# The second mixer with part of GpSimd's elementwise work on other engines, and the router in column tiles

## The chip, the cores and the metric

The kernel runs on one core of a Trainium2 chip: five engines (TensorE for matmuls, here PE; VectorE, DVE; ScalarE, ACT; GpSimd, POOL; SyncE, SP, which only issues transfers) work in order, each on its own queue, and wait for one another by semaphores. The metric is device microseconds (us) for one execution, lower is better.

## The reference

Two layers of a diffusion block on 512 latent rows and 256 context rows of width 1024. Layer 0 mixes by latent attention and retention, layer 1 by a two-directional RWKV-7 recurrence and a window attention; after each mixer a router picks rows for 16 experts (expert choice) and a gated feed-forward layer adds their outputs. What the change touches:

```python
p = p + mu * (0.5 * (left_neighbour + right_neighbour) - p)   # rwkv_features, per column of p
w = -softplus(-(w0[d] + tanh(wl) @ w2[d])) - 0.5
a = sigmoid(a0[d] + al @ a2[d])
key = k * (1 + (a - 1) * k_a)
S = S * dec + (S @ -kk) (kk * a)^T + v k^T                      # one step of the recurrence
aff = softmax(h @ w_router); gate, idx = top_k(aff^T, 64 or 32)   # 16 experts
```

The recurrence is computed in chunks of 64 steps; inside a chunk a 64x64 unit triangular matrix T = I + G is inverted by doubling blocks, once per head.

## The kernel before

Order of the work: mixer 0, router 0, experts of layer 0, mixer 1, router 1, experts of layer 1. Weights of the experts stream through a ring of 2 MB slots. The framework places the instructions of each engine by its own planner, with tile releases as waits, except on PE in the expert layers, where the order is that of the program.

Mixer 1 (mixer1, from L791) is one static loop that steps many generators in turn:

- `front` projects the input: for each block of 128 columns of the weight matrix, `weights` (L863) loads 512 KB, ACT rounds it to a high part (L871), and DVE or POOL in turn subtracts it to get the low part (L872); `project` (L919) does 24 matmuls (L926). `shifted` (L929) turns the result `pb` into the shifted feature: ACT copies it between two zero columns (L937), POOL adds the left and right neighbours (L939), DVE or ACT scales by 1-mu (L941, L943), DVE adds hm times the sum (L944). It runs 25 times, on 256 or 512 columns.
- `features` (L950), 12 times on 256 columns, makes decays and keys: ACT's tanh (L972), on POOL the step to a sigmoid (L975), the factor of the key (L1009) and its product with k (L1014), on DVE a scan (L996) and the products that go to DRAM (L1021 to L1031), from where they are loaded again.
- `prep` (L1295), 24 times (2 directions, 2 halves of the heads, 6 row tiles), solves the triangular systems of four chunks. DVE masks the Gram matrix into `GA` (L1331) and adds I into `Thbd` (L1338); POOL makes `Ttbd` = GA - I (L1341) and the first masked block `Zbd` (L1357); DVE transposes (L1356) and masks (L1358) X; then come five levels of matmul, copy and transpose (L1285, L1366 to L1384). At the end the residual is formed on PE (L1398, L1399: T X + I for each of four chunks) and used to correct the inverse; POOL rounds a copy to half precision (L1393).
- `chain` (L1416), 48 steps in four independent strands, carries the state: POOL multiplies the old state by the decay (L1428), PE, DVE, ACT (L1443) and PE make the update, DVE joins them (L1452).
- `win_attend`, `finish` and `projected` (L1556 to L1563) follow in the same loop.

The router (`route_open` L1654, `route_tile` L1664) norms a row tile, transposes and scales it (`ht`), and forms 16 logits with 8 matmuls, each with 128 rows of `ht` as the stationary operand and 16 columns moving. The router's weights `wr` lie in a pool that lives through the whole kernel:

```python
        lg = self.bank("lg")
        for k in range(8):
            nc.tensor.matmul(lg[:, 0:16], ht[:, k], self.rwr[:, k], start=k == 0, stop=k == 7)   # L1688
        nc.vector.tensor_copy(self.lgt[:, t], lg[:, 0:16])
```

Of the kernel before, what the change touches and what calls it, by code (L numbers as in the profile page):

```python
# [11 lines left out]
F32 = mybir.dt.float32  # L12
# [3 lines left out]
AF = mybir.ActivationFunctionType  # L16
# [83 lines left out]
class Kern:  # L100
# [690 lines left out]
    def mixer1(self):  # L791
# [69 lines left out]
        def weights():  # L861

            while len(cut) < 2 and (queue or order):  # L863
# [8 lines left out]
                (nc.vector if len(order) % 2 else nc.gpsimd).tensor_tensor(w[:, 1], raw, w[:, 0].bitcast(F32), OP.subtract)  # L872
# [9 lines left out]
        nc.gpsimd.tensor_copy(id16[:, 0:128], self.ident)  # L882
        nc.gpsimd.tensor_copy(id16[:, 128:192], id64)
# [46 lines left out]
        def shifted(blk, a, out):  # L930

            n = a[0].shape[2]
            for pb in project(a, 1024 // n):
                yield
            pd = fo.tile([128, NLAT + 2], F32, name="pd")
            nc.gpsimd.memset(pd[:, 0:n + 2:n + 1], 0.0)
            nc.scalar.activation(pd[:, 1:n + 1], pb, AF.Copy)  # L937
            s = fo.tile([128, NLAT], F32, name="sh")
            nc.gpsimd.tensor_tensor(s[:, :n], pd[:, 0:n], pd[:, 2:n + 2], OP.add)  # L939
            if n < NLAT or blk % 2:  # L940
                nc.vector.tensor_scalar(out, pb, om[:, blk:blk + 1], None, OP.mult)  # L941
            else:
                nc.scalar.activation(out, pb, AF.Copy, scale=om[:, blk:blk + 1])  # L943
            nc.vector.scalar_tensor_tensor(out, s[:, :n], hm[:, blk:blk + 1], out, OP.mult, OP.add)  # L944
# [6 lines left out]
        def features(p, t0, kp, rp, vp, low):  # L951
# [13 lines left out]
            for (lst, wt, src, bias) in ((sig, w2, tl, w0v), (aa, a2, al, a0v)):  # L965
# [7 lines left out]
                if lst is sig:  # L973
                    for d in dirs:
                        nc.gpsimd.tensor_scalar(sig[d], sig[d], 0.5, 0.5, OP.mult, OP.add)  # L975
# [31 lines left out]
            for d in dirs:  # L1007
                nc.vector.scalar_tensor_tensor(q0[d], aa[d], 1.0, kk, OP.add, OP.mult)
                nc.gpsimd.tensor_scalar(aa[d], aa[d], hka[:, p:p + 1], oka[:, p:p + 1], OP.mult, OP.add)  # L1009
# [3 lines left out]
            for d in dirs:  # L1013
                nc.gpsimd.tensor_tensor(aa[d], aa[d], kp, OP.mult)  # L1014
# [280 lines left out]
        def prep(sl, st_, d, u, j):  # L1295
# [44 lines left out]
            for h in range(2):  # L1340
                nc.gpsimd.tensor_tensor(Ttd[h], GA[0:64, :, h], id64[0:64, None, :].to_broadcast([64, 4, 64]),  # L1341
                                        OP.subtract)
# [12 lines left out]
            for h in range(2):  # L1355
                nc.vector.transpose(X[hd[h]], Thd[h])  # L1356
                nc.gpsimd.tensor_tensor(Zd[h], Thd[h], lev(0, 1 - d)[hd[h]], OP.mult)  # L1357
# [58 lines left out]
        def chain(d, u, j):  # L1416
# [7 lines left out]
            for c in ((0, 1) if d == 0 else (1, 0)):  # L1424
                n0 = Ns[c] = N0[d, u]
                dec = PL[:, d, 2 * u:2 * u + 2, 2 * tt + c]
                n0s = rf.tile([128, 2, 64], F32, name="n0s", tag=f"s{d}{u}", bufs=1)
                nc.gpsimd.tensor_tensor(n0s, n0, dec[:, :, None].to_broadcast([128, 2, 64]), OP.mult)  # L1428
# [22 lines left out]
                for p in range(2):  # L1451
                    nc.vector.scalar_tensor_tensor(N1[:, p], a2_(pn)[:, p], dec[:, p:p + 1], n0s[:, p], OP.mult, OP.add)  # L1452
# [201 lines left out]
    def route_open(self, l):  # L1654
# [497 lines left out]
```

## Time and profile before

| | |
|---|---|
| median of 3 runs | 2968.59 us (2965.43 to 2972.07) |
| the profiled execution | 2972.21 us, its span 2970.4 us |
| busy: PE, DVE, ACT, POOL | 2660.2 us (90%), 1322.9 us (45%), 742.6 us (25%), 471.4 us (16%) |
| mean granted TensorE clock | 0.954 |
| chain that ended last, by engine | PE 64%, DMA 19%, DVE 9%, POOL 3%, ACT 3% |

Busy shares are averages over stages with different limits. The chain that ended last is followed back from the last instruction, at each step to what released it; time of an engine on it is time that set the end. "issue" in it is time without a wait that the profile shows. A matmul of 4-byte operands leaves two records in the trace.

### The profile page before, as it was taken

Reading aid. Unit: us, or ns where it says so; the run is one execution under the profiler, and the core shown is the slowest. Engines: PE = TensorE matmul, PEld = TensorE weight load, DVE = VectorE, ACT = ScalarE, POOL = GpSimd, SP = SyncE. Lnnn points to the kernel's source line nnn. Section 1 sums busy time; section 2 is a strip of 40 time slices with the busy share of each in tenths; the row PEclk is TensorE's granted clock in tenths of the full one; section 3 lists DMA queues with packets and bytes.
Section 4 is the critical chain, followed back from the end, with each engine's and each line's share of the span. In section 5 each row is a group of like instructions: output and inputs, shape, how many; then the busy total and the mean of one; then the engine's idle time right before and its main releaser. Section 6 shows DMA issues by size and latency. Waiting matters only on the chain.

```text
span 2970.4 us, 47837 instructions
## 1 busy us (share of the span) xinstructions
PE 2660.2 (90%) x19606; PEld 1535.4 (52%) x19606; DVE 1322.9 (45%) x3546; ACT 742.6 (25%) x1718; POOL 471.4 (16%) x591
## 2 busy tenths in 40 slices
PE   7999999799999999999878878799987987888886
PEld 4787776544444444444466656587653332333322
DVE  4323665444234334322475777677654332223312
ACT  3212444211111111101354544366321111101111
POOL 2332003200000000000283553411210000000000
PEclk9999999799999999999987988899987999999999
DMA  9765001488988988988642233310349999999997
GB/s 329 244 246 175 27 12 57 172 333 353 371 356 355 371 345 367 365 355 355 216 126 73 86 108 120 111 32 28 118 184 377 426 427 427 427 426 427 426 427 314
DMA packets 176587, 779.47 MB, mean 262 GB/s; under 512 B 24327, under 2 KB 110768, under 8 KB 133488
## 3 DMA queue, kind: packets, MB, share of 16 engines
q1 hardware_dynamic: 169200, 752.31, 64.5%
q0 software_dynamic: 3872, 12.52, 1.2%
q10 hardware_dynamic: 3296, 11.58, 1.0%
q8 instruction: 155, 2.54, 0.4%
q14 instruction: 64, 0.52, 0.1%
HBM read 745.68 MB, written 30.67 MB: 261 GB/s over the span
## 4 chain that ended last, share of the span: by engine, by line
PE 64%; DMA 19%; DVE 9%; POOL 3%; ACT 3%; issue 2%; SPq 0%; POOLq 0%; ACTq 0%; DVEq 0%
PE gu L1924 13%; PE ydn L1992 9%; DMA wd<-in_moe_w_down_dram 8%; DMA we<-in_moe_w_gate_up_dram 8%; PE guc L1937 6%; PE ydc L1996 3%; PE pj L926 3%; PE pj L411 2%; PE pj L412 2%; PE pj L413 2%; PE op L774 2%; PE op L1556 2%; PE adap L231 2%; PE sc L593 1%; PE scp L1816 1%
## 5 line engine op out<-in xcount | busy, mean ns | idle before, releaser
L1924 PE MATMUL gu<-we,xs 128*64 128x512 f32 x3072 | 687.9, 597 | 83.5 <-DMA we<-in_moe_w_gate_up_dram 83.4
L1924 PEld LDWEIGHTS gu<-we,xs 128*64 128x64 f32 x3072 | 216.7, 137 | 520.5 <-issue 408.5
L1992 PE MATMUL ydn<-wd,uT 128*64 128x512 f32 x1536 | 351.8, 600 | 14.3 <-DMA wd<-in_moe_w_down_dram 13.7
L1930 DVE TENSOR_TENSOR sg<-gu,sg 64x512 f32<-64x512 f32 x96 | 66.5, 693 | 458.4 <-ACT sg L1929 457.8
L1929 ACT ACTIVATE sg<-gu 64x512 f32<-64x512 f32 x96 | 56.8, 592 | 846.3 <-PE gu L1924 846.3
L1776 POOL DMA_INDIRECT xg<-xnd,idx x22 | 20.9, 952 | 1246.6 <-DVE gate L1781 1186.0
L1992 PEld LDWEIGHTS ydn<-wd,uT 128*64 128x64 f32 x1536 | 107.9, 137 | 205.3 <-issue 187.0
L1937 PE MATMUL guc<-we,xs 128*32 128x256 f32 x3072 | 172.6, 380 | 0.0
L926 PE MATMUL pj<-aL,wblk 128*128 128x512 f32 x504 | 158.1, 448 | 0.0
L1937 PEld LDWEIGHTS guc<-we,xs 128*32 128x32 f32 x3072 | 96.4, 110 | 68.4 <-issue 7.5
L411 PE MATMUL pj<-ah,wblk 128*128 128x384 f32 (+1 forms) x320 | 109.5, 343 | 1.4 <-ACT ah L380 1.4
L926 PEld LDWEIGHTS pj<-aL,wblk 128*128 128x128 f32 x504 | 99.0, 210 | 18.4
L412 PE MATMUL pj<-al,wblk 128*128 128x384 f32 (+1 forms) x320 | 107.9, 338 | 0.0
L413 PE MATMUL pj<-ah,wblk 128*128 128x384 f32 (+1 forms) x320 | 107.4, 336 | 0.0
L1819 DVE TENSOR_TENSOR x<-scp,x 128x512 f32<-128x512 f32 x144 | 92.3, 684 | 30.3 <-PE scp L1817 29.4
L1996 PE MATMUL ydc<-wd,uTc 128*32 128x256 f32 x1536 | 90.6, 380 | 1.4 <-DMA wd<-in_moe_w_down_dram 1.4
L1906 DVE COPY uTc<-utc 128x128 f32<-128x128 f32 x48 | 14.0, 291 | 172.6 <-PE utc L1904 172.1
L2046 DVE TENSOR_TENSOR yp<-ydn,gbc 64x512 f32<-64x512 f32 x64 | 44.1, 689 | 103.8 <-PE ydn L1992 103.3
L1796 DVE TENSOR_SCALAR xs<-xst,gm,modT 128x128 f32<-128x128 f32 (+1 forms) x88 | 34.8, 397 | 118.9 <-PE xst L1788 115.7
L1900 ACT ACTIVATE uT<-utp 128x256 f32<-128x256 f32 x96 | 36.0, 375 | 159.4 <-PE utp L1899 158.6
L1382 DVE STREAM_TRANSPOSE Zbd<-X 64x256 f16<-64x256 f16 x144 | 62.7, 436 | 24.2 <-ACT X L1376 21.8
L1996 PEld LDWEIGHTS ydc<-wd,uTc 128*32 128x32 f32 x1536 | 47.6, 110 | 43.9 <-issue 15.2
(421 smaller groups left out, 4630.4 us busy)
## 6 DMA issues: line engine op xcount, KB each, us to landing
we<-in_moe_w_gate_up_dram SPq DMA_DIRECT2D x192, 2048.0 KB, 13.5
wd<-in_moe_w_down_dram SPq DMA_DIRECT2D x95, 2048.0 KB, 11.8
adaw<-in_ada_w_dram SPq DMA_DIRECT2D x48, 1024.0 KB, 6.5
wraw<-in_od_w_in_dram SPq DMA_DIRECT2D x33, 512.0 KB, 4.2
wraw<-in_ev_w_in_dram SPq DMA_DIRECT2D x19, 512.0 KB, 6.8
fb<-B SPq DMA_DIRECT2D x24, 256.0 KB, 2.5
BK<-fb SPq DMA_DIRECT2D x24, 256.0 KB, 3.0
xnd<-xn ACTq DMA_DIRECT2D x10, 512.0 KB, 4.7
```

Of the source, the lines that this page charges most:

```text
L231: nc.tensor.matmul(pb[32 * j:32 * j + 32], self.spad[:, k, :], w[:, 512 * j:512 * j + 512], start=k == 0, stop=k == 7, tile_position=(0, 3 ...
L411: nc.tensor.matmul(pb[:m, :384], w[:, 0, k, 0:m], ah[k][:, t], start=k == 0, stop=False)
L412: nc.tensor.matmul(pb[:m, :384], w[:, 0, k, 0:m], al[k][:, t], start=False, stop=False)
L413: nc.tensor.matmul(pb[:m, :384], w[:, 1, k, 0:m], ah[k][:, t], start=False, stop=k == 7)
L926: nc.tensor.matmul(pb[:, :n], w[:, i, k], a[j][:, k], start=k + i + j == 0, stop=k == 7 and i == 1)
L1382: nc.vector.transpose(Zd[h], X[hd[h]])
L1819: nc.vector.tensor_tensor(xs, pb, xs, OP.add)
L1924: nc.tensor.matmul(gu[64 * j:64 * j + 64, :], g.xs[:, k, 64 * a:64 * a + 64], ws[j][k], start=k == 0, stop=k == 7, tile_position=(0, 64 * j))
L1930: nc.vector.tensor_tensor(sg, gu[64:128], sg, OP.mult)
L1937: nc.tensor.matmul(guc[32 * j:32 * j + 32, 0:256], q.xs[:, k, 32 * a4:32 * a4 + 32], ws[j // 2][k][:, 256 * (j % 2):256 * (j % 2) + 256], ...
L1992: nc.tensor.matmul(y[64 * h:64 * h + 64, :], uT[:, f], wt[i][:, 512 * h:512 * h + 512], start=f == 0, stop=f == 11, tile_position=(0, 64 * h))
L1996: nc.tensor.matmul(yc[32 * j:32 * j + 32, 0:256], uTc[:, f], wt[i][:, 256 * j:256 * j + 256], start=f == 0, stop=f == 11, tile_position=(0 ...
```

## The change

Every elementwise operation of mixer 1 that stood on POOL in the loops above goes to DVE or ACT, or falls away: the low part of the weights always on DVE; the neighbour sums as two multiply-adds of DVE straight from the matmul's bank; the two affine steps of `features` on ACT and the product on DVE; `Ttbd` a plain copy on ACT, with the subtraction of I done by PE; the masked `Zbd` on DVE; the half-precision copy on ACT; the decayed state no longer formed, since (new + old) is multiplied by the decay. The router's 8 matmuls become 8 in column tiles, 32 wide, with `ht` moving, and one that adds the four tiles up and transposes; its weights move to the router's own pool.

```diff
-                (nc.vector if len(order) % 2 else nc.gpsimd).tensor_tensor(w[:, 1], raw, w[:, 0].bitcast(F32), OP.subtract)
+                nc.vector.tensor_tensor(w[:, 1], raw, w[:, 0].bitcast(F32), OP.subtract)
...
+        minus = cpl.tile([128, 128], F32, name="minus")
+        nc.scalar.activation(minus, self.ident, AF.Copy, scale=-1.0)
...
-            pd = fo.tile([128, NLAT + 2], F32, name="pd")
-            nc.gpsimd.memset(pd[:, 0:n + 2:n + 1], 0.0)
-            nc.scalar.activation(pd[:, 1:n + 1], pb, AF.Copy)
-            s = fo.tile([128, NLAT], F32, name="sh")
-            nc.gpsimd.tensor_tensor(s[:, :n], pd[:, 0:n], pd[:, 2:n + 2], OP.add)
-            if n < NLAT or blk % 2:
-                nc.vector.tensor_scalar(out, pb, om[:, blk:blk + 1], None, OP.mult)
-            else:
-                nc.scalar.activation(out, pb, AF.Copy, scale=om[:, blk:blk + 1])
-            nc.vector.scalar_tensor_tensor(out, s[:, :n], hm[:, blk:blk + 1], out, OP.mult, OP.add)
+            nc.scalar.activation(out, pb, AF.Copy, scale=om[:, blk:blk + 1])
+
+            for o, s in ((1, 0), (0, 1)):
+                o = out[:, o:n - 1 + o]
+                nc.vector.scalar_tensor_tensor(o, pb[:, s:n - 1 + s], hm[:, blk:blk + 1], o, OP.mult, OP.add)
...
-                        nc.gpsimd.tensor_scalar(sig[d], sig[d], 0.5, 0.5, OP.mult, OP.add)
+                        nc.scalar.activation(sig[d], sig[d], AF.Identity, bias=half, scale=0.5)
...
-                nc.gpsimd.tensor_scalar(aa[d], aa[d], hka[:, p:p + 1], oka[:, p:p + 1], OP.mult, OP.add)
+                nc.scalar.activation(aa[d], aa[d], AF.Identity, bias=oka[:, p:p + 1], scale=hka[:, p:p + 1])
...
-                nc.gpsimd.tensor_tensor(aa[d], aa[d], kp, OP.mult)
+                nc.vector.tensor_tensor(aa[d], aa[d], kp, OP.mult)
...
-                nc.gpsimd.tensor_tensor(Ttd[h], GA[0:64, :, h], id64[0:64, None, :].to_broadcast([64, 4, 64]),
-                                        OP.subtract)
+                nc.scalar.activation(Ttd[h], GA[0:64, :, h], AF.Copy)
...
-                nc.gpsimd.tensor_tensor(Zd[h], Thd[h], lev(0, 1 - d)[hd[h]], OP.mult)
+                nc.vector.tensor_tensor(Zd[h], Thd[h], lev(0, 1 - d)[hd[h]], OP.mult)
...
-            nc.gpsimd.tensor_copy(Zc, Zf)
+            nc.scalar.activation(Zc, v3(pz), AF.Copy)
...
+            nc.tensor.matmul(v3(pf), id16[:, 0:128], id16[:, None, 128:192].to_broadcast([128, 4, 64]), start=True,
+                             stop=False)
+            nc.tensor.matmul(v3(pf), minus, X, start=False, stop=False)
             for c in range(4):
-                o = pf[:, 64 * c:64 * c + 64]
-                nc.tensor.matmul(o, Tt[:, c], X[:, c], start=True, stop=False)
-                nc.tensor.matmul(o, id16[:, 0:128], id16[:, 128:192], start=False, stop=True)
+                nc.tensor.matmul(pf[:, 64 * c:64 * c + 64], Tt[:, c], X[:, c], start=False, stop=c == 3)
...
-                nc.gpsimd.tensor_tensor(n0s, n0, dec[:, :, None].to_broadcast([128, 2, 64]), OP.mult)
...
-                for p in range(2):
-                    nc.vector.scalar_tensor_tensor(N1[:, p], a2_(pn)[:, p], dec[:, p:p + 1], n0s[:, p], OP.mult, OP.add)
+                nc.vector.tensor_tensor(N1, a2_(pn), n0, OP.add)
+                nc.vector.tensor_tensor(N1, N1, dec[:, :, None].to_broadcast([128, 2, 64]), OP.mult)
...
-        self.rwr = self.small.tile([128, 8, 16], F32, name="wr", tag="wr", bufs=1)
-        nc.gpsimd.dma_start(self.rwr, io["moe_router"][l].rearrange("(k p) n -> p k n", p=128))
+        self.rwr = self.rtw.tile([128, 8, 32], F32, name="wr", bufs=1)
+        nc.gpsimd.memset(self.rwr[:, :, 16:32], 0.0)
+        nc.gpsimd.dma_start(self.rwr[:, :, 0:16], io["moe_router"][l].rearrange("(k p) n -> p k n", p=128))
...
+        lp = self.bank("lgp")
+        for i in range(2):
+            for j in range(4):
+                nc.tensor.matmul(lp[32 * j:32 * j + 32, 0:128], self.rwr[:, 4 * i + j], ht[:, 4 * i + j], start=i == 0,
+                                 stop=i == 1, tile_position=(0, 32 * j))
+        ls = self.rtw.tile([128, 128], F32, name="ls")
+        nc.scalar.activation(ls, lp[:, 0:128], AF.Copy)
+        yield
+
         lg = self.bank("lg")
-        for k in range(8):
-            nc.tensor.matmul(lg[:, 0:16], ht[:, k], self.rwr[:, k], start=k == 0, stop=k == 7)
+        nc.tensor.matmul(lg[:, 0:16], ls, self.rsum, start=True, stop=True)
         nc.vector.tensor_copy(self.lgt[:, t], lg[:, 0:16])
```

`rsum` is four 16-column slices of the identity added up by DVE in `route_open`.

## Rows read from the trace of the kernel before

**Rows 1.** Busy time by stretch: PE, PEld, DVE, ACT, POOL, clock, DMA share, GB/s.
```profile
1456.00:1560.00 104.00, 72.79 (x426) 63.53 (x424) 75.17 (x139) 57.97 (x120) 74.65 (x104) 0.83 0.51 150
1560.00:1910.00 350.00, 290.11 (x2396) 221.59 (x2397) 239.43 (x533) 151.90 (x372) 160.79 (x219) 0.87 0.31 91
1910.00:2110.00 200.00, 178.16 (x2004) 152.60 (x2003) 137.43 (x416) 118.90 (x354) 41.15 (x65) 0.93 0.23 73
...
2400.00:2500.00 100.00, 84.00 (x400) 31.98 (x398) 27.14 (x80) 10.97 (x23) 0.94 (x1) 1.00 1.01 427
```

**Rows 2.** The chain that ended last, mixer 1, 1456 to 2206 us, by line.
```profile
by line: PE pj L926 10.4%; issue 5.4%; PE op L1556 4.5%; PE pe L1398 3.8%; DVE Thbd L1338 3.4%; PE sw L1200 3.2%; PE po L1236 3.1%; DVE Zbd L1382 2.5%; DVE X L1356 2.0%; PE px L1285 1.7%; POOL wblk L872 1.7%; PE pf L1285 1.7%; PE gv L1406 1
```

**Rows 3.** The same, 1456 to 1560 us.
```profile
by line: PE pj L926 13.6%; issue 8.7%; POOL wblk L872 7.4%; POOL ssq L987 4.9%; ACT wblk L871 4.7%; SPq L1312 4.6%; PE lw L969 3.7%; POOL lo L1014 3.5%; POOL lo L1009 3.4%; DVE raw L817 3.0%; DMA BK<-fb 3.0%; POOL lo L975 2.9%; DVE wblk L87
```

**Rows 4.** The same, 1560 to 1910 us.
```profile
by line: PE pj L926 18.2%; issue 5.6%; PE pe L1398 4.1%; DVE Thbd L1338 3.8%; DVE Zbd L1382 2.8%; POOL lo L1009 2.3%; DVE X L1356 2.2%; DVE cl L996 2.1%; DMA BK<-fb 2.1%; PE gv L1406 2.0%; PE pf L1285 2.0%; PE px L1285 2.0%; DMA fa<-A 1.9%;
```

**Rows 5.** The same, 1640 to 1760 us.
```profile
by line: PE pj L926 11.0%; POOL lo L1009 6.6%; DMA fa<-A 5.7%; issue 5.3%; POOL lo L1014 4.6%; DVE cl L996 4.3%; ACT lo L972 3.2%; DVE Zbd L1382 2.7%; PE lw L969 2.7%; PE pe L1398 2.7%; POOL sh L939 2.6%; DVE Thbd L1338 2.6%; POOL ssq L987 
```

**Rows 6.** Groups of POOL by form, mixer 1: busy us, mean ns, idle before.
```profile
L872 POOL TENSOR_TENSOR wblk<-wraw,wblk 128x1024 fp32r<-128x1024 f32 x17 | 42.0, 2470 | 14.4 <-ACT wblk L871 14.2
...
L1009 POOL TENSOR_SCALAR lo<-lo,hka,oka 128x256 f32<-128x256 f32 x24 | 22.4, 937 | 3.0 <-DVE t L1008 3.0
...
L1014 POOL TENSOR_TENSOR lo<-lo,ko 128x256 f32<-128x256 f32 x24 | 18.2, 772 | 0.6
```

**Rows 7.** Groups of DVE and ACT by form, mixer 1.
```profile
L1338 DVE TENSOR_TENSOR Thbd<-GA,m 64x256 f16<-64x256 f32 x48 | 35.9, 747 | 0.9
...
L872 DVE TENSOR_TENSOR wblk<-wraw,wblk 128x1024 fp32r<-128x1024 f32 x16 | 20.9, 1307 | 2.5 <-ACT wblk L871 2.3
...
L1005 DVE TENSOR_TENSOR lo<-cl,lo 128x256 f32<-128x256 f32 x24 | 9.4, 423 | 0.1
...
L944 DVE SCALAR_TENSOR_TENSOR ro<-sh,hm,ro 128x512 f32<-128x512 f32 x4 | 3.0, 746 | 0.5 <-POOL sh L939 0.5
...
L980 ACT ACTIVATE kq<-ko,vT 128x256 f32<-128x256 f32 x12 | 6.1, 511 | 3.4 <-DVE ko L944 3.4
```

**Rows 8.** Timeline of DVE in two of the 24 preps: start, us, instruction.
```profile
1883.73 1.70 DVE L1338 TENSOR_TENSOR Thbd<-GA,m 64x256 f16<-64x256 f32 x2
...
1886.74 0.28 DVE L1358 TENSOR_TENSOR X<-X,lev 128x256 f16<-128x256 f16 x1
...
1918.12 0.86 DVE L1338 TENSOR_TENSOR Thbd<-GA,m 64x256 f16<-64x256 f32 x2
```

**Rows 9.** Matmuls on the chain, in order of time: start, us, line, records.
```profile
1489.59 0.45 PE lw L969 x2
...
2081.51 1.06 PE po L1236 x10
...
2099.42 0.48 PE pe L1398 x2
```

**Rows 10.** Who waited for whom in mixer 1: us in total, times, longest.
```profile
ACT UV L1443 <- PE pu L1440: 52.5, 24, 6.6
...
PE pf L1285 <- DVE X L1358: 23.2, 16, 3.1
```

**Rows 11.** The chain in router 0 and in the experts of layer 0.
```profile
505.97 1.69 PE lg L1688 x16
...
1284.41 3.59 PE ydc L1996 x64
1288.00 3.58 PE ydn L1992 x16
```

**Rows 12.** Router 1: its weights' landing time, timeline of the last L1512 and first L1688.
```profile
DMA to landing us min/median/max: 7.4/7.8/8.2
...
2205.03 0.69 DVE L1512 TENSOR_TENSOR rwT<-Fb,rwT 128x512 f32<-128x512 f32 x1 [1.37 <-POOL rwT L1510]
...
2220.37 3.42 PE L1688 MATMUL lg<-wr,ht 128*128 128x16 f32 x30
```

More of the change, by code (lines that the diff above doesn't have):

```diff
@@ L882, in mixer1 @@
         nc.gpsimd.tensor_copy(id16[:, 0:128], self.ident)
+        minus = cpl.tile([128, 128], F32, name="minus")
+        nc.scalar.activation(minus, self.ident, AF.Copy, scale=-1.0)
+        half = cpl.tile([128, 1], F32, name="half")
+        nc.gpsimd.memset(half, 0.5)
         nc.gpsimd.tensor_copy(id16[:, 128:192], id64)
@@ L1426, in chain @@
                 dec = PL[:, d, 2 * u:2 * u + 2, 2 * tt + c]
-                n0s = rf.tile([128, 2, 64], F32, name="n0s", tag=f"s{d}{u}", bufs=1)
-                nc.gpsimd.tensor_tensor(n0s, n0, dec[:, :, None].to_broadcast([128, 2, 64]), OP.mult)
                 pa = self.bank("an")
@@ L1659, in route_open @@
         self.rgm, self.rsh = self.gmod(l, 1)
-        self.rwr = self.small.tile([128, 8, 16], F32, name="wr", tag="wr", bufs=1)
-        nc.gpsimd.dma_start(self.rwr, io["moe_router"][l].rearrange("(k p) n -> p k n", p=128))
+        self.rwr = self.rtw.tile([128, 8, 32], F32, name="wr", bufs=1)
+        nc.gpsimd.memset(self.rwr[:, :, 16:32], 0.0)
+        nc.gpsimd.dma_start(self.rwr[:, :, 0:16], io["moe_router"][l].rearrange("(k p) n -> p k n", p=128))
+        self.rsum = self.rtw.tile([128, 16], F32, name="rsum", bufs=1)
+        nc.vector.tensor_tensor(self.rsum, self.ident[:, 0:16], self.ident[:, 32:48], OP.add)
+        for j in (2, 3):
+            nc.vector.tensor_tensor(self.rsum, self.rsum, self.ident[:, 32 * j:32 * j + 16], OP.add)
         self.lgt = self.small.tile([128, 6, 16], F32, name="lgt", tag="lgt", bufs=1)
```

## The prediction

> **What bounds the kernel now.** I read the page first, then the busy time by stretch, the chain of waits, the groups by form, and the timeline where a group's mean hid two kinds of instruction. The first thing to see is that the stages have different limits. The experts of layer 1 are bound by transfers: the DMA engines are busy all the time at 427 GB/s while PE idles 16% (the last of [rows 1]). The experts of layer 0 are bound by PE, whose matmuls follow each other without a gap [rows 11]. So what ends earlier in router 0 or in mixer 1 moves the end one for one, and what ends earlier in router 1 only as far as the weight stream starts earlier.
>
> Mixer 1, 1456 to 2206 us, is bound by no single engine: PE is busy 70 to 89% of each stretch. POOL is unlike its share on the page: in the first 104 us it is busy 74.65 us, as much as DVE [rows 1], and its subtraction of weights, powers and key factors are a good part of the chain [rows 3]. Until 1910 it stays there [rows 4, 5]; after that it is idle most of the time.
>
> The second thing is in the timeline. The two additions of L1338 take 1.70 us together while POOL forms `Ttbd`, and 0.86 us where POOL does not read at that moment [rows 8]; their mean of 747 ns [rows 7] is mostly the slow kind. So POOL costs twice, on the chain by itself and by what it does to DVE.
>
> **The parts and their cost.** Shares of the chain are turned into us by the length of their stretch.
>
> 1. Low part of the weights: 17 subtractions go from POOL (2.47 us) to DVE (1.307 us) [rows 6, 7]. POOL's are 1.7% of 750 us on the chain [rows 2], 12.8 us or 5.2 instructions; 5.2 x 1.16 = 6.0 us less. DVE has 22.2 us more to do.
> 2. Key factor L1009: on the chain 3.4% of 104 and 2.3% of 350 us [rows 3, 4], 11.6 us or 12.4 of its 24 instructions (0.937 us [rows 6]). On ACT with two operands per partition the price is unseen; the nearest row is ACT's square of the same shape with one, 0.511 us [rows 7]. I take that: 12.4 x 0.426 = 5.3 us less. The bounds are 0 (as slow as on POOL) and the whole 11.6.
> 3. Product with k, L1014: 3.5% of 104 and 4.6% of 120 us [rows 3, 5], 9.2 us or 11.9 instructions of 0.772 us [rows 6]; on DVE the same shape takes 0.423 us [rows 7]: 11.9 x 0.35 = 4.2 us less.
> 4. The sigmoid step L975, 2.9% of 104 us [rows 3], is about as long on ACT as on POOL: nothing. The power L987, 4.9% of 104 us or 5.1 us [rows 3], stays on POOL but no longer queues behind steps 1 to 3; I take 3 us less, between 0 and 5.
> 5. Neighbour sums: POOL's addition goes, and DVE gets a second multiply-add of 0.75 us [rows 7] in 25 blocks; 17 of these lose a scaling on DVE, and ACT scales instead of copying. On the chain the addition is 2.6% of 120 us, 3 us [rows 5]. Taken at nothing; between 3 us less and, were the 8 extra multiply-adds all paid, 6 more. The bank of the matmul is held until DVE is done with it; the loop has eight, and late is then the next block's matmul.
> 6. `Thbd` with POOL out of the way: 3.4% of 750 us [rows 2] is 25.5 us, 34 instructions of 747 ns; at 0.43 us [rows 8] they take 14.7: 10.8 us less. Bounds: 0, if something else stretches them, and 12.7, if all on the chain were of the slow kind.
> 7. `Zbd` on DVE: two half-precision products stand between the transposes and X of L1358, for which PE waited in 16 preps [rows 10]. The nearest row is L1358 itself, 0.28 us [rows 8]: 16 x 0.56 = 9.0 us more, between 0 (the planner puts them behind) and 14 (all 24). [...]
> 8. `Ttbd` as a copy, the half-precision copy of Z: 48 + 24 more instructions on ACT, at up to 0.51 us 37 us of work. Cover: ACT arrives early and waits, 52.5 us in all, for the state updates [rows 10], and has 81 us idle in 1910 to 2110 [rows 1]. Nothing; if the cover is gone, what is late next is the copy of the state's update, and up to 37 us are paid.
> 9. Residual on PE: before, four times 0.48 us on the chain [rows 9] and the four additions of I between them; after, four 64-column matmuls (five take 1.06 [rows 9], so 0.85), one of 256 columns (0.45 [rows 9]) and one in half precision (at most half of that): 1.52 against 1.92. L1398 is 3.8% of 750 us [rows 2], 28.5 us or 14.8 preps: 6 us less, between 0 and 12.
> 10. The state: two multiply-adds become an addition and a product of about the same sum; the POOL step was beside PE. Nothing either way.
> 11. Router 0: 8 matmuls take 1.69 us on the chain [rows 11]. In tiles 32 wide, 32 matmuls of 256 columns take 3.59 us [rows 11], so 8 of 128 columns 0.45 to 0.90, and the last one 0.21: I take 0.9, 0.8 us less for each of six tiles, 4.8 us. The rows show no gap at the change from 32-wide to 64-wide tiles: 1284.41 + 3.59 = 1288.00 [rows 11]. [...]
> 12. Router 1: 15 matmuls, 3.42 us [rows 12], stand on PE ahead of the last projection, whose end lets the second half of the weight stream go. Two tiles at 0.9 us: 1.5 us less. The load of `wr` moves: it was made long before, now its memory lies under tiles of `finish` and is free after 2205.7 [rows 12]; with a clearing on POOL and 8.2 us to land it is there at about 2215, 5 us before its first use at 2220.4. On POOL's queue it stands by the row tiles' powers, at under 1 us; SP's queue is not touched.
>
> Sum: -6.0 - 5.3 - 4.2 - 3 - 10.8 + 9.0 - 6 - 4.8 - 1.5 = -32.6 us. Against the profiled execution's 2972.2 that is 2939.6; the median of the runs lies 3.6 us lower: **2936**.
>
> **The rivals.**
> A. DVE takes POOL's place (next late). For it: DVE is busy 72% of the first stretch and 68% of the second [rows 1]. Against it: step 6 gives it 15 us back. Then steps 1 to 4 give half of their 18.5 us: 2936 + 9 = 2945, and 2955 if nothing of them is left.
> B. More than the sum: the first stretch runs on POOL's queue in series, and moved work goes to two engines side by side; a denser PE also sees less of the lower clock (0.83 and 0.87 granted [rows 1]). If the first stretch shrinks by 20% and the second by 10%, 56 us, with the routers' 6 and 4 later: 2903.
> C. Slower. Mechanism: DVE's queue in front and prep. Steps 1, 3, 5 and 7 bring it 22 + 10 + 6 + 13 = 52 us; if half of that lands on the path, and the gains of steps 1 to 6 do not come because `Thbd` stays long and other waits end where POOL's did, the end moves by 26 - 12 (steps 9, 11, 12) = +14: 2982. It decides once DVE's 139 us of idle time up to 1910 cannot take the added work; the idle is scattered over waits for PE and ACT, so this is not excluded.
> D. The change does little: the planner puts the moved work where it delays as much as it frees, only the routers gain: 2962.
>
> **How the numbers follow.** The sum 0.50, A 0.20, B 0.14, D 0.06, C 0.10. The range leaves out C and the ends of B and D: 2897 to 2966. A measurement of this kernel can tell about 0.2%, 6 us, from no change: faster is the sum, A, B and part of D, 0.84; the same 0.07; slower 0.09.
>
> **What would show it.** Right: `Thbd` near 430 ns in all 48; POOL's busy time in 1456 to 1910 falling from 235 us to below 100; the stretch before the window attention shorter by 20 us or more, the attention's by a few; the router's matmuls near 0.9 us; the tail of transfers as long as before. Wrong: DVE above 80% in the front (A, C); L1443 and L1376 waiting in ACT's queue behind copies (step 8); `lg` waiting for the load of `wr` (step 12).

## The result, and the profile after

The changed kernel takes 2930.06 us (median of 4 runs, 2928.15 to 2933.29) against 2968.86 before (4 runs): ratio 0.9871, interval 0.9854 to 0.9888, or 38.8 us less. The forecast was 2936 in 2897 to 2966, faster: it held. How the sum was put together held far less, and the experiments are about that.

The profiled execution spans 2928.8 us, 41.6 less than the one before:

| stretch | before | after | difference |
|---|---|---|---|
| start to the end of experts 0 (last `ydn`) | 1451.10 | 1450.53 | -0.6 |
| mixer 1, to the end of the last `yt` | 750.55 | 712.46 | -38.1 |
| tail of the mixer and router 1, to the first `gu` | 55.88 | 51.42 | -4.5 |
| experts 1 and the rest | 712.87 | 714.39 | +1.5 |

The last row holds the tail of transfers and is about as long as before. Busy time by stretch of mixer 1 after, to be read beside [rows 1]: to the first `gr`, to the first `sw`, to the first `op`, to the last `yt`, and the whole. Columns as in [rows 1].

```profile
1450.53:1545.89 95.36, 68.27 (x444) 60.28 (x444) 75.41 (x158) 66.10 (x142) 32.17 (x50) 0.93 0.56 163
1545.89:1887.80 341.91, 287.42 (x2424) 220.47 (x2425) 245.57 (x616) 180.45 (x448) 34.54 (x52) 0.90 0.36 104
1887.80:2069.49 181.69, 172.40 (x1958) 148.10 (x1958) 128.31 (x413) 123.80 (x369) 0.00 (x0) 0.97 0.20 63
2069.49:2162.99 93.50, 85.20 (x848) 51.65 (x847) 58.42 (x136) 25.16 (x70) 10.20 (x7) 0.94 0.30 103
1450.53:2162.99 712.46, 613.29 (x5671) 480.50 (x5671) 507.71 (x1323) 395.51 (x1027) 76.91 (x109) 0.93 0.34 101
```

The whole of mixer 1 before, in the same view:

```profile
1451.10:2201.65 750.55, 629.77 (x5695) 491.74 (x5695) 515.82 (x1226) 355.15 (x914) 298.62 (x415) 0.89 0.31 93
```

Three things are to be seen. POOL falls from 299 to 77 us, 67 of them ahead of the first `sw`. (Not everything on POOL moved: the power and the broadcast of the norm in `features`, the low part of the latents and a few more stay there.) PE is idle for 99.2 us (712.46 - 613.29) in place of 120.8. And PE is busy 16.5 us less with nearly the same matmuls, at a mean granted clock of 0.93 in place of 0.89. DVE, which was given POOL's work, is not busier: 507.71 us against 515.82. By stretch, the way to the first `sw` is 35.3 us shorter (472.55 to 437.27) and the attention, up to the first `op`, 5.5 shorter, as the prediction would have it; the rest of the mixer is 2.6 longer.

Why DVE is not busier stands in its groups by form (the answers to [rows 6 to 8]; the columns are busy us, mean ns, idle before):

```profile
L872 DVE TENSOR_TENSOR wblk<-wraw,wblk 128x1024 fp32r<-128x1024 f32 x33 | 40.1, 1219 | 1.1 <-ACT wblk L871 0.9
L1354 DVE STREAM_TRANSPOSE X<-Thbd 64x256 f16<-64x256 f16 x48 | 21.1, 439 | 1.5
L1337 DVE TENSOR_TENSOR Thbd<-GA,m 64x256 f16<-64x256 f32 x48 | 19.8, 412 | 0.9
L1355 DVE TENSOR_TENSOR Zbd<-Thbd,lev 64x256 f16<-64x256 f16 x48 | 11.8, 245 | 0.0
L1020 DVE TENSOR_TENSOR A<-kk,lo 128x256 f32<-128x256 f32 x24 | 10.0, 418 | 1.4 <-DMA fa<-A 1.4
L1029 DVE SCALAR_TENSOR_TENSOR B<-t,cl 128x256 f32<-128x256 f32 x24 | 10.0, 416 | 0.0
...
L1340 ACT ACTIVATE Ttbd<-GA 64x256 f32<-64x256 f32 x48 | 19.9, 415 | 31.2 <-DVE GA L1330 30.8
L1008 ACT ACTIVATE lo<-lo,oka,hka 128x256 f32<-128x256 f32 x24 | 13.1, 591 | 0.1
```

Before, in the same view, the transposes and the features' products were

```profile
L1356 DVE STREAM_TRANSPOSE X<-Thbd 64x256 f16<-64x256 f16 x48 | 21.1, 439 | 1.5
L1021 DVE TENSOR_TENSOR A<-kk,lo 128x256 f32<-128x256 f32 x24 | 17.5, 727 | 3.1 <-DMA fa<-A 2.9
L1030 DVE SCALAR_TENSOR_TENSOR B<-t,cl 128x256 f32<-128x256 f32 x24 | 14.6, 609 | 1.1 <-DMA fb<-B 1.1
```

`Thbd` went from 747 to 412 ns, as step 6 said (430). But `A` and `B`, to which the change does nothing, got shorter as well, by 7.5 and 4.6 us. Their means hide two kinds: before, the median `A` takes 426 ns and the longest 2574; after, 418 and 428. The transposes, which have one input, did not move: 439 ns in both. So some of DVE's instructions with two inputs were held up beside POOL's work, in more places than the prediction priced; e3 below puts one such case back.

The chain of mixer 1 after (the answer to [rows 2]):

```profile
by line: PE pj L930 12.7%; PE op L1553 6.5%; issue 5.6%; PE sw L1199 4.4%; PE po L1235 3.6%; PE gr L1325 3.3%; PE pe L1398 3.2%; PE pu L1437 2.1%; PE gv L1405 2.1%; PE pe L1396 2.1%; PE pn L1445 2.1%; PE ptw L1223 2.0%; PE pf L1284 2.0%; PE
```

`Thbd` (3.4% before) and POOL's `wblk` (1.7%) are no longer among the first; the list is PE's own work.

Router 1, matmuls on PE in order (the answer to [rows 12]):

```profile
2181.16 1.07 PE L1694 MATMUL lgp<-ht,wr 128*32 128x128 f32 x30
2182.16 1.12 PE L1553 MATMUL op<-wo,rwT 128*128 128x512 f32 x2
```

Two tiles take 1.07 us in place of 3.42. The load of `wr` was issued at 2167.7 and took 7.8 us, so it lay there 5.7 us ahead. The merged rows leave no gap between the 32-wide tiles and the full-width `op`, but the starts do: groups of four tiles start every 0.11 us, the last of them at 2181.95, and the `op` at 2182.16, 0.2 us later; it also takes 0.70 us where the others take 0.59. So the change from the tiles to the full width costs some 0.2 us here; whether the change itself or the load of the next weights, which also starts at 2182.16, makes it is not told apart.

### The profile page after: what moved, and what is told of

Its sections match the earlier page's. It is cut to its first block, busy times and chain, and to the rows that moved or that the text cites. A ratio compares the mean times of both kernels' runs of the same rounds, so it can differ in the third digit from the quotient of the medians.

```text
span 2928.8 us, 47636 instructions
## 1 busy us (share of the span) xinstructions
PE 2640.5 (90%) x19602; PEld 1511.1 (52%) x19602; DVE 1316.9 (45%) x3649; ACT 785.5 (27%) x1841; POOL 250.3 (9%) x287
## 4 chain that ended last, share of the span: by engine, by line
PE 68%; DMA 18%; DVE 7%; ACT 3%; issue 2%; POOL 1%; SPq 1%; ACTq 0%; POOLq 0%; DVEq 0%
PE gu L1937 14%; PE ydn L2005 9%; DMA wd<-in_moe_w_down_dram 9%; DMA we<-in_moe_w_gate_up_dram 7%; PE guc L1950 6%; PE pj L930 3%; PE ydc L2009 3%; PE op L1553 2%; PE pj L411 2%; PE op L774 2%; PE pj L412 2%; PE pj L413 2%; PE adap L231 1%; PE sc L593 1%; PE scp L1829 1%
## 5 line engine op out<-in xcount | busy, mean ns | idle before, releaser
L930 PE MATMUL pj<-aL,wblk 128*128 128x512 f32 x504 | 143.8, 421 | 0.0
L930 PEld LDWEIGHTS pj<-aL,wblk 128*128 128x128 f32 x504 | 93.1, 197 | 16.8
L1806 ACT ACTIVATE xs<-xst,modT,gm 128x128 f32<-128x128 f32 (+1 forms) x88 | 38.3, 448 | 119.8 <-DVE xs L1809 118.7
```

The costliest lines, as they stand in the source:

```text
L930: nc.tensor.matmul(pb[:, :n], w[:, i, k], a[j][:, k], start=k + i + j == 0, stop=k == 7 and i == 1)
```

## The experiments

Two theories stood against each other. **Contention**: POOL's instructions stretch DVE's, so what counts is what runs beside what. **Queue**: POOL's results were waited for, so what counts is which of its instructions lay on the chain. All ratios are to the kernel before, as it ran beside that experiment (medians 2971.1 to 2971.6, against 2968.9 beside the changed kernel).

### The two halves

e1 is the kernel before with the hunks of `route_open` and `route_tile` alone (the router in tiles); e2 is the changed kernel with these two hunks taken back.

> The kernel before with the router in tiles and nothing else of the change. If the gain of router 0 carries to the end (the forecast), the time falls by 4.8 us there and 1.5 us in router 1, to about 2963 by the median (6 us less). If experts 0 give it back, as the trace of the changed kernel suggests (first expert matmul 4.1 us earlier, end of experts 0 only 0.6 us earlier), the end of experts 0 moves by under 1 us and the whole by 3 to 4 us, all of it in router 1. The place to read it: the first gu, the guc that follow it, and the last ydn of experts 0.

> The changed kernel with the router of before: the mixer's part of the change alone. If experts 0 give router 0's gain back, it is 3 to 4 us above the changed kernel, about 2933.5, and the mixer is as long as there (723 to 724 us between the last ydn and the last rwT). If the router's tiles are worth their 6 us, about 2936.

e1: 2965.04 us, 0.9983 (0.9973 to 0.9993), 5 us less. e2: 2938.42 us, 0.9887 (0.9872 to 0.9902), 32.6 us less. The halves add up to the whole.

The theory that experts 0 give the router's gain back rested on one execution of before, and it falls. It came from this (PE's columns and the clock, in windows of 4 us behind the first expert matmul), before:

```profile
600.00:604.00 4.00, 1.31 (x10) 0.86 (x8) 3.97 (x20) 1.23 (x3) 0.00 (x0) 1.00 0.10 39
604.00:608.00 4.00, 3.94 (x64) 2.67 (x68) 3.24 (x14) 1.13 (x3) 1.08 (x2) 1.00 0.24 63
```

after:

```profile
600.00:604.00 4.00, 3.24 (x24) 2.24 (x28) 2.38 (x8) 1.83 (x4) 0.91 (x1) 0.58 0.00 0
604.00:608.00 4.00, 4.00 (x48) 1.95 (x44) 3.96 (x21) 0.00 (x0) 0.18 (x1) 0.57 0.50 121
```

The changed kernel runs at a granted clock of 0.58 and 0.57 here, near the lower level (0.50), the one before at the upper (1.00). But e2, with the router of before, has a low stretch there too (0.75 and 0.50 in 604 to 612). Over all traces of this study, the 4 with the old router end experts 0 at 1451.10, 1456.47, 1453.25 and 1455.34, mean 1454.0; the 10 with the new one at 1447.4 to 1451.5, mean 1449.8. So 4.2 us come through, and the execution of before was a lucky one there. From the last `yt` to the first `gu` the old router takes 55.3 to 55.9 us and the new one 50.4 to 52.6: 3.9 less by the means. That is 8 us by the traces; the runs say 5 (2 to 8).

### POOL beside DVE, unread

e3 adds to the changed kernel the 48 subtractions that POOL did before, into a tile that nobody reads.

```diff
+            junk = new([64, 4, 64], "jk")
+            for h in range(2):
+                nc.gpsimd.tensor_tensor(junk, GA[0:64, :, h], id64[0:64, None, :].to_broadcast([64, 4, 64]),
+                                        OP.subtract)
```

e4 makes the copy `Ttbd` on POOL:

```diff
-                nc.scalar.activation(Ttd[h], GA[0:64, :, h], AF.Copy)
+                nc.gpsimd.tensor_copy(Ttd[h], GA[0:64, :, h])
```

> The changed kernel with 48 subtractions back on POOL where Ttbd was formed (same operands, same shape), but into a tile that nobody reads: no other engine waits for POOL, so what it costs is what POOL's traffic does to the others. Contention theory: Thbd goes from 412 ns back to about 740 ns in all 48, 16 us of DVE time, of which 34 of 48 instructions lie on the chain: the mixer 11 us longer, about 2941. Rival (POOL cost only through the waits for its own results): Thbd stays under 450 ns and the time within 3 us of the changed kernel's 2930.

> The changed kernel with Ttbd copied on POOL and not on ACT; the residual stays in its new form. Contention theory: as long as with the unread subtractions beside it, about 2941, Thbd near 740 ns. Rival (the 20 us that the copies cost ACT are what is on the path): ACT without them is quicker, the time falls to 2920 to 2928. If both hold they offset, and the time is near 2930 with Thbd long.

e3: 2955.59 us, 0.9950 (0.9932 to 0.9968): by the medians 25.5 us above the changed kernel, and nobody reads what POOL makes there. Its groups:

```profile
L1337 DVE TENSOR_TENSOR Thbd<-GA,m 64x256 f16<-64x256 f32 x48 | 37.2, 776 | 0.9
L1358 DVE STREAM_TRANSPOSE X<-Thbd 64x256 f16<-64x256 f16 x48 | 21.1, 439 | 1.5
L1020 DVE TENSOR_TENSOR A<-kk,lo 128x256 f32<-128x256 f32 x24 | 10.0, 417 | 1.7 <-DMA fa<-A 1.6
...
L1343 POOL TENSOR_TENSOR jk<-GA,m 64x256 f32<-64x256 f32 x48 | 36.9, 770 | 306.0 <-DVE GA L1330 280.3 <-DVE wm L1212 23.8
```

`Thbd` alone of these is stretched, by 17.4 us in all. PE waits longer for X, which is made from it; the changed kernel first, then e3:

```profile
PE pf L1284 <- DVE X L1356: 17.2, 10, 2.6
...
PE pf L1284 <- DVE X L1360: 28.8, 16, 3.2
```

That is 11.6 us more, the size expected. One load of weights on PE waited 1.7 us for an unread subtraction, through the buffer that it reads; the rival, that POOL costs only where its results are waited for, cannot make 25 us of that and is excluded. But 25 us is more than twice the 11 expected, and more than the whole stretch.

e4: 2932.62 us, 0.9884 (0.9867 to 0.9901), the same as the changed kernel, and `Thbd` is not near 740 ns: none of the expectations is met.

```profile
L1337 DVE TENSOR_TENSOR Thbd<-GA,m 64x256 f16<-64x256 f32 x48 | 23.4, 487 | 0.9
...
L1340 POOL COPY Ttbd<-GA 64x256 f32<-64x256 f32 x48 | 21.8, 455 | 300.0 <-DVE GA L1330 298.7
```

POOL's copy costs `Thbd` 75 ns on average; its subtraction costs 364. And taking the copies off ACT gains nothing: ACT's cover held (step 8). So `Ttbd` on POOL need not cost anything; the long instruction does. What makes the difference is told by the ends. A pair on DVE and the pair on POOL beside it in e3, the same in e4, and one `A` in e6 (below) beside POOL's subtraction of weights:

```profile
1962.76 1.71 DVE L1337 TENSOR_TENSOR Thbd<-GA,m 64x256 f16<-64x256 f32 x2
1962.60 1.59 POOL L1343 TENSOR_TENSOR jk<-GA,m 64x256 f32<-64x256 f32 x2 [28.89 <-DVE GA L1330]
...
1948.64 1.02 DVE L1337 TENSOR_TENSOR Thbd<-GA,m 64x256 f16<-64x256 f32 x2
1948.46 0.93 POOL L1340 COPY Ttbd<-GA 64x256 f32<-64x256 f32 x2 [29.06 <-DVE GA L1330]
...
1516.92 2.58 DVE L1020 TENSOR_TENSOR A<-kk,lo 128x256 f32<-128x256 f32 x1
1516.58 2.65 POOL L872 TENSOR_TENSOR wblk<-wraw,wblk 128x1024 fp32r<-128x1024 f32 x1 [3.66 <-ACT wblk L871]
```

In each, POOL's began first and DVE's ends 0.27 to 0.28 us after POOL's end (1964.19 and 1964.47, 1949.39 and 1949.66, 1519.23 and 1519.50), though POOL's instructions take 0.46, 0.8 and 2.65 us. So DVE's instruction is held here until POOL's is done, and the price is what is left of POOL's when DVE's comes; that the copy has one input matters, as far as these ends show, only in that it is shorter. In the kernel before, the two `Thbd` end 0.27 to 0.29 us after POOL's two subtractions in 15 of the 24 preps. The transposes, with one input, are not held beside POOL's `Zbd` in the kernel before: there two of them run from 1885.46 to 1886.37 and `Zbd` from 1885.22 to 1886.69, and the mean of all, 439 ns, is that of the changed kernel.

### The granted clock

Where do e3's other us come from? The whole of mixer 1 in e3:

```profile
1449.19:2187.70 738.51, 625.83 (x5671) 490.88 (x5671) 526.06 (x1323) 396.11 (x1027) 114.44 (x157) 0.90 0.32 98
```

Against the changed kernel PE is idle 13.5 us longer (112.7) and busy 12.5 us longer, with the same 5671 matmul records at 0.90 in place of 0.93. A pause of PE can be paid twice: as the pause, and as matmuls at the lower level (0.50) after it. In the kernel before, the same matmuls of the residual (L1398 and L1399 for four chunks) take 1.12 us at a granted clock of 1.00 (2075.22 to 2076.34) and 2.28 us at 0.50 (2098.14 to 2100.42). One place with such a pause in the kernel before, by windows of 2 us (columns as in [rows 1]):

```profile
1771.10:1773.10 2.00, 0.14 (x1) 0.00 (x0) 1.91 (x6) 1.67 (x3) 1.85 (x4) 1.00 0.34 97
...
1775.10:1777.10 2.00, 0.00 (x0) 0.00 (x0) 2.00 (x2) 0.00 (x0) 1.92 (x3) 0.50 0.37 131
...
1787.10:1789.10 2.00, 2.00 (x33) 1.68 (x29) 1.05 (x4) 0.56 (x2) 0.00 (x0) 0.50 0.00 0
...
1791.10:1793.10 2.00, 2.00 (x19) 1.44 (x18) 0.42 (x2) 0.93 (x3) 0.68 (x1) 1.00 0.76 262
```

PE is idle, the clock falls to 0.50, and matmuls that fill PE again still run at 0.50 until shortly before 1791. The runs that left no trace agree for e3: the mean granted clock of its 6 executions is 0.957 to 0.961, that of the changed kernel's 4 is 0.961 to 0.965.

This can be worked out for each trace. Read the granted clock in windows of 2 us: of the 376 in mixer 1 before, 270 read 1.00, the upper level, 61 read 0.50, the lower, and 45 lie between and count in proportion. By the 1.12 and 2.28 us above, PE's busy time at the lower level would have taken half at the upper. So length = idle + half of the busy time at the lower level + PE's work at the upper:

| kernel | us (median) | mixer 1 | PE idle | half of busy at the lower level | work at the upper |
|---|---|---|---|---|---|
| before | 2968.9 | 750.6 | 120.8 | 68.0 | 561.8 |
| e11 weights alone | 2970.6 | 745.1 | 119.4 | 65.5 | 560.2 |
| e1 router alone | 2965.0 | 745.5 | 120.3 | 65.2 | 560.0 |
| e10 residual alone | 2958.3 | 735.3 | 110.6 | 52.2 | 572.5 |
| e5 residual undone | 2958.9 | 743.0 | 112.4 | 70.7 | 559.9 |
| e3 POOL beside, unread | 2955.6 | 738.5 | 112.7 | 54.0 | 571.8 |
| e12 more moved | 2950.0 | 731.8 | 101.0 | 61.3 | 569.5 |
| e6 weights undone | 2948.0 | 734.4 | 106.1 | 58.8 | 569.5 |
| e9 sums undone | 2946.4 | 728.4 | 103.9 | 51.8 | 572.7 |
| e2 router undone | 2938.4 | 716.0 | 94.5 | 51.3 | 570.2 |
| e4 `Ttbd` on POOL | 2932.6 | 715.0 | 103.2 | 40.9 | 570.9 |
| e7 features undone | 2931.7 | 716.3 | 97.7 | 47.0 | 571.6 |
| e8 `Zbd` behind | 2930.9 | 713.1 | 101.6 | 40.0 | 571.5 |
| changed kernel | 2930.1 | 712.5 | 99.2 | 42.3 | 571.0 |

The last column takes two values, 560 to 562 with the old form of the residual and 569 to 573 with the new one, so the split is sound to some 3 us. It is that of the one profiled execution, which lies up to 5 us from the median (e2 at 2943.7, e6 at 2952.2). The change took 21.6 us of pauses, 25.7 us of lower clock, and paid 9.2 us of PE work.

### The parts undone one by one

All losses here are of medians, against the changed kernel's 2930. By the ratios, which allow for the kernel before being 2 to 3 us slower beside the experiments, e3, e5, e6, e9 and e12 lose 2 to 5 us less, and e7 gains 4; each such difference carries some 7 us of uncertainty. e8, which ran beside e5 to e7 and is no different from the changed kernel, gives them 28, 17 and 1 by the medians. e5 takes the residual's hunks back:

```diff
-                nc.scalar.activation(Ttd[h], GA[0:64, :, h], AF.Copy)
+                nc.gpsimd.tensor_tensor(Ttd[h], GA[0:64, :, h], id64[0:64, None, :].to_broadcast([64, 4, 64]),
+                                        OP.subtract)
...
-            nc.tensor.matmul(v3(pf), minus, X, start=False, stop=False)
...
+                nc.tensor.matmul(o, Tt[:, c], X[:, c], start=True, stop=False)
+                nc.tensor.matmul(o, id16[:, 0:128], id16[:, 128:192], start=False, stop=True)
```

> The changed kernel with T minus I formed by POOL's subtraction again and the residual as four plus four matmuls again; everything else of the change stays. Contention theory: as with the unread subtractions beside it, Thbd near 776 ns and about 23 us lost, plus the 6 us forecast for the residual on PE: about 2959; if the residual's new form is worth nothing, about 2953. By the sizes of the prediction (10.8 for Thbd, 6 for the residual) 2947.

2958.89 us, 0.9955 (0.9941 to 0.9969): 29 us lost, as the contention theory had it. Against e3 the old residual is worth 3 us, less than the intervals can tell.

e6 takes the weights' hunk back:

```diff
-                nc.vector.tensor_tensor(w[:, 1], raw, w[:, 0].bitcast(F32), OP.subtract)
+                (nc.vector if len(order) % 2 else nc.gpsimd).tensor_tensor(w[:, 1], raw, w[:, 0].bitcast(F32), OP.subtract)
```

> The changed kernel with every second low part of the weights on POOL again (17 of 33 subtractions). The prediction's step: 6 us lost, about 2936, all of it ahead of the window attention. Contention theory: POOL's subtraction of 1024 columns also slows DVE while it runs, so 6 us or more, and DVE's instructions beside it longer than in the changed kernel. Rival (the blocks are cut ahead of their use and the weights cost nothing): 2930.

2948.04 us, 0.9915 (0.9901 to 0.9930): 18 us lost by the medians (13 by the ratios), two to three times the step.

```profile
L1337 DVE TENSOR_TENSOR Thbd<-GA,m 64x256 f16<-64x256 f32 x48 | 19.8, 413 | 1.0
...
L1029 DVE SCALAR_TENSOR_TENSOR B<-t,cl 128x256 f32<-128x256 f32 x24 | 15.3, 636 | 3.0 <-DMA fb<-B 3.0
L1020 DVE TENSOR_TENSOR A<-kk,lo 128x256 f32<-128x256 f32 x24 | 14.3, 596 | 3.3 <-DMA fa<-A 3.3
```

`A` and this `B` are long again, `Thbd` is not. It is a few of them: the medians are 418 ns, the longest 2584 and 2582, about the length of POOL's subtraction, as in the `A` shown above. A matmul of `project` waits for POOL's weights only once, for 1.7 us. PE's pauses grow by 6.9 us, the clock's share by 16.5.

e7 takes the features' hunks back:

```diff
-                        nc.scalar.activation(sig[d], sig[d], AF.Identity, bias=half, scale=0.5)
+                        nc.gpsimd.tensor_scalar(sig[d], sig[d], 0.5, 0.5, OP.mult, OP.add)
...
-                nc.scalar.activation(aa[d], aa[d], AF.Identity, bias=oka[:, p:p + 1], scale=hka[:, p:p + 1])
+                nc.gpsimd.tensor_scalar(aa[d], aa[d], hka[:, p:p + 1], oka[:, p:p + 1], OP.mult, OP.add)
...
-                nc.vector.tensor_tensor(aa[d], aa[d], kp, OP.mult)
+                nc.gpsimd.tensor_tensor(aa[d], aa[d], kp, OP.mult)
```

> The changed kernel with the features' steps on POOL again: the decay's half and half, the key factor and its product with k. The prediction's steps 2 to 4: 5.3 + 4.2 + 3 = 12.5 us lost, about 2942.5. Contention theory: the product with k has two inputs, so the scan, A and both B go from 416 to 680 ns back to 605 to 755 ns, another 5 us or so: 2945 to 2950. Rival (POOL, now otherwise idle, does these as fast as the path wants them): within 3 us of 2930.

2931.67 us, 0.9857 (0.9837 to 0.9877): nothing lost, the queue's 12.5 us are not there.

```profile
L1029 DVE SCALAR_TENSOR_TENSOR B<-t,cl 128x256 f32<-128x256 f32 x24 | 11.9, 494 | 0.8 <-DMA fb<-B 0.8
...
L1008 POOL TENSOR_SCALAR lo<-lo,hka,oka 128x256 f32<-128x256 f32 x24 | 21.2, 888 | 25.3 <-DVE t L1007 25.3
L1013 POOL TENSOR_TENSOR lo<-lo,ko 128x256 f32<-128x256 f32 x24 | 19.5, 821 | 0.7
```

POOL is slower at each of these than the engines that now do it (ACT 591 ns and DVE 441 in the changed kernel), and `B` is a little longer, yet PE is idle no longer than in the changed kernel (97.7 us). The reading that fits is that with POOL's other work gone the features are ready ahead of use; the features' part alone on the kernel before was not run.

e8 keeps all of the change and puts the two `Zbd` products behind the product for X:

```diff
                 nc.vector.transpose(X[hd[h]], Thd[h])
-                nc.vector.tensor_tensor(Zd[h], Thd[h], lev(0, 1 - d)[hd[h]], OP.mult)
             nc.vector.tensor_tensor(X, X, lev(0), OP.mult)
+            for h in range(2):
+                nc.vector.tensor_tensor(Zd[h], Thd[h], lev(0, 1 - d)[hd[h]], OP.mult)
```

> The changed kernel with the two products for Zbd put behind the product for X in DVE's order, so that X and PE's first product no longer wait for them. By step 7 of the prediction they stand in the path of most preps: 24 x 0.49 = 11.8 us of DVE time at most, about two thirds of it on the chain, so 6 to 9 us less: 2921 to 2924. Rival (the planner hides them, or Zbd is then late for the second product of PE): 2930 within 3 us.

2930.88 us, 0.9863 (0.9847 to 0.9878): the same. The `Zbd` products (245 ns each in the changed kernel, where step 7 took the 280 of [rows 8]) cost nothing in front of X. What they cost on POOL was not tried.

e9 takes the hunk of `shifted` back:

```diff
+            nc.scalar.activation(pd[:, 1:n + 1], pb, AF.Copy)
...
+            nc.gpsimd.tensor_tensor(s[:, :n], pd[:, 0:n], pd[:, 2:n + 2], OP.add)
...
-            for o, s in ((1, 0), (0, 1)):
...
+            nc.vector.scalar_tensor_tensor(out, s[:, :n], hm[:, blk:blk + 1], out, OP.mult, OP.add)
```

> The changed kernel with the neighbour sums as before: ACT copies into a padded tile, POOL adds the neighbours, DVE does one multiply-add (and, in 17 of 25 blocks, the scaling). The prediction's step 5 forecast nothing (-3 to +6): 2930, 2933 at most. Contention theory: POOL's two-input addition of 512 columns (about 1.07 us) slows DVE beside it and makes each block's chain longer, PE waits more and its granted clock falls from 0.93: 2936 to 2945. Rival (the sums cost the change something, which would explain why the parts undone one by one add up to more than the whole): 2915 to 2925.

2946.41 us, 0.9918 (0.9904 to 0.9932): 16 us lost by the medians, 14 by the ratios. The rival that the sums cost the change something falls. The contention theory's number holds, but little of its mechanism is to be seen:

```profile
L1342 DVE TENSOR_TENSOR Thbd<-GA,m 64x256 f16<-64x256 f32 x48 | 20.6, 429 | 0.9
...
L1035 DVE TENSOR_TENSOR B<-lo,cl 128x256 f32<-128x256 f32 x24 | 10.8, 450 | 0.0
```

One `Thbd` of 48 and a few others are held up, 4 us or so of DVE's time in all. The split gives 4.7 us more pauses, 9.5 us more at the lower clock and 1.7 us more work. What the old form of the sums does to PE, by contention or by its longer way over ACT, POOL and DVE, is not told apart.

### The parts alone, and more of the same

e10 is the kernel before with the hunks of the residual (e5's diff, the other way round) and of the state update; e11 the kernel before with the weights' hunk alone (e6's diff, the other way round). e12 goes on from the changed kernel, with e8's order and

```diff
-            nc.gpsimd.tensor_copy(nrm, ssq[:, 4:8, None].to_broadcast([128, 4, 64]))
+            nc.scalar.activation(nrm, ssq[:, 4:8, None].to_broadcast([128, 4, 64]), AF.Copy)
...
-                (nc.vector if t < 2 or k0 else nc.gpsimd).tensor_tensor(l, r, h.bitcast(F32), OP.subtract)
+                nc.vector.tensor_tensor(l, r, h.bitcast(F32), OP.subtract)
...
-            nc.gpsimd.tensor_tensor(ro, ro, F[:, 0], OP.add)
+            nc.vector.tensor_tensor(ro, ro, F[:, 0], OP.add)
```

> The kernel before with the residual's part of the change alone: Ttbd copied by ACT, the residual with minus X and I on PE; and the state update without POOL's step, which frees the memory that minus needs. Weights, features, neighbour sums, Zbd and the router stay as before. If parts add up, it gains what undoing it lost, 29 us: about 2942. If the parts overlap (what one takes off the path another also takes off), less: 2950 to 2960. By the prediction's sizes (10.8 + 6) 2954.

2958.31 us, 0.9962 (0.9947 to 0.9976): 13 us less by the medians, not 29.

> The kernel before with all low parts of the weights on DVE and nothing else of the change. By the prediction's step 1: 6 us less, 2965. If the 18 us that undoing it cost in the changed kernel are there in this one too: 2953. If the other POOL work keeps the path as it is and DVE has 22 us more to do: 2971 or above.

2970.61 us, 0.9999 (0.9990 to 1.0007): nothing, where undoing it cost 18.

> The changed kernel with more of POOL's rest taken off it: the broadcast of the norm to ACT (0.75 us on POOL, 7.8 us of the chain in 9 pieces), the low part of the latents' input and the addition of the bonus in the last part to DVE, and the products for Zbd behind the one for X. If what is left of POOL still costs the path, 4 to 8 us less than the changed kernel: 2922 to 2926. If PE's own work sets the end by now (the granted clock already 0.93), within 3 us of 2930.

2949.99 us, 0.9932 (0.9918 to 0.9946): 20 us worse than the changed kernel, against both expectations. The whole of mixer 1 by windows, and the moved broadcast among ACT's groups:

```profile
1449.26:2181.01 731.75, 630.79 (x5671) 495.08 (x5671) 516.43 (x1329) 399.65 (x1039) 62.87 (x90) 0.90 0.32 99
```

```profile
L988 ACT ACTIVATE nrm<-ssq 128x256 f32<-128x256 f32 x12 | 5.0, 416 | 10.4 <-POOL ssq L986 10.4
```

The broadcast is quicker (416 ns, on POOL 745), and PE is idle 101.0 us, 2 us more than in the changed kernel. But the same 5671 matmuls take 17.5 us more, at 0.90: in the windows of 2 us the clock lies under 0.75 in 20 stretches of the mixer in place of 15. Nearly all of the loss is in the clock, and all 6 executions show it (mean granted clock 0.955 to 0.959, the changed kernel's 0.961 to 0.965). Which of the four edits brings it was not tried; `Zbd` behind X alone (e8) does not.

## Why the prediction was right

It was right in its sign and its sum (32.6 forecast, 38.8 measured), and right in the mechanism that weighs most, POOL holding up DVE. That the sum came so near is in good part luck: the terms of 12.5 (the features), 6 (the residual) and -9 us (`Zbd`) came out at about nothing, while undoing the weights, `Thbd` and the sums cost far more than their terms.

- **Step 6**, `Thbd` uncontended: the mechanism and the 412 ns were right; the term was mis-sized. It was priced at 10.8 us, and PE's wait for X does grow by 11.6 us in e3; but putting only the contention back costs 25. What was left out is the lower clock that came with PE's pauses, 11.7 us more of it in e3.
- **Step 1**, the weights: 6 forecast. Alone 0 (e11), undone 18 by the medians (e6). There is no such number by itself.
- **Steps 2 to 4**, the features: 12.5 forecast, 0 to 2 when undone (e7). They were on the chain [rows 3, 5]; with the other parts of the change in place they are not worth moving. That POOL's full queue had put them there is a reading that no run tested.
- **Step 5**, the sums: nothing forecast; undone 16 (e9). The chain showed POOL's addition at 3 us; 9.5 us of what e9 loses are lower clock, which a chain of waits does not show.
- **Step 7**, `Zbd`: 9 us more forecast; putting X ahead of them gains nothing (e8). PE waits for X less than before (17.2 us in place of 23.2 in [rows 10]), though X now comes behind two more instructions.
- **Step 8**: right, the cover held (e4).
- **Step 9**, the residual: -6 forecast. The row taken for the old form, 0.48 us at 2099 us [rows 9], lies where the granted clock was 0.62 (2097 to 2101.5), and 0.50 in the residual itself (2098.14 to 2100.42). At the upper level (1.00), at 2075 us, the four pairs follow each other every 0.28 us and take 1.12 us together (2075.22 to 2076.34); the new form takes 1.47 at the same level (2034.97 to 2036.44), the addition of I not counted (on PE from 2034.08, 0.11 us until the next matmul). So the row was read at the wrong clock and the sign was wrong: the new form is 9 us more PE work in the table, and e5 against e3 shows nothing gained.
- **Steps 11 and 12**, the routers: 6.3 forecast, 5 (2 to 8) measured by e1. Router 0's 4.8 is 4.2 over the traces. Router 1's 1.5 was too little, 3.9: two tiles give 1.9 us (3.42 and 0.45 before, 1.07, 0.41 and 0.51 after), and the tiles behind the last projection are shorter too. The load was 5.7 us early, 5 forecast. That step 11 saw no pause at a change of the tiling was a reading of merged rows: the 32-wide tiles of [rows 11] start in groups of four every 0.22 us, and the first 64-wide one starts 0.33 us after the last group.

Of the rivals, A (DVE takes POOL's place) does not happen: DVE is busy less. In B stood the words that a denser PE sees less of the lower clock, with 0.14: of the mixer's 38.1 us in the traces, 25.7 are lower clock, though B's 56 us did not come. C had the right resource, DVE's queue, but its condition, that `Thbd` stays long, is not met.

The parts don't add up. Undone one by one they cost 29, 18, 2 and 16 us, 65 in all (48 by the ratios), where the mixer's whole gain is 33 (e2). The sum of four such differences is uncertain by some 20 us; the firmer sign is that done alone two of them bring 13 and 0, in place of 29 and 18, and the 13 has the state's update in it. `Zbd`, the half-precision copy and the state's update were not undone by themselves. In the table each kernel with one part left on POOL (e3, e5, e6, e9; not e7) has both more pauses and more time at the lower clock, and e11, with one part taken off, has hardly less of either than before. But pauses alone do not set the clock: e4, e8, e9 and e12 all have 101 to 104 us of them, and 41, 40, 52 and 61 us in the column of the lower level. What pattern brings the clock down stays open.

## What to carry over

Before moving work off an engine, look for what that engine stretches: compare the same instruction's duration with and without the neighbour, its longest as well as its mean, and look at instructions that the change does not touch. What POOL holds up in the places shown, it holds until its own instruction ends (DVE's ends 0.27 to 0.28 us after it), so a short one may stay: with POOL's copy of 455 ns (e4) the kernel takes 2932.6 us, with its subtraction of 770 ns (e3) 2955.6. In this mixer, where PE is busy 84 to 86% of the time with a granted clock under 1, the sum of chain terms (26 us) came out below what the edits did together (33) and was no guide to what one did alone: split each trace into pauses, busy time at the lower level, and work. And read a matmul's price where the clock is the same as where it will be used.

## What was not expected of the hardware

POOL's subtraction made DVE's two-input instruction of the same size take 776 in place of 412 ns (e3), and a copy on POOL 487 (e4): in the three places shown DVE's instruction ends 0.27 to 0.28 us after POOL's, whatever POOL's takes. Some 14 us of POOL's work moved to other engines, with two instructions in another order (e12), cost 20 us through TensorE's clock, with 2 us more idle time on TensorE. No kernel here beat the changed one by more than the intervals.
